# Inputs laid out feature-major, and Strassen over all 16 k tiles with uneven halves of the tokens, in a hybrid encoder layer on one core

## The chip, the cores and the metric

The kernel runs on one core of a Trainium2 chip. Its time is the device time of one execution in microseconds (us), as the median over several executions. The profile describes one execution, taken by the hardware profiler. PE is the matrix engine (PEld its weight loads), DVE the vector engine, ACT the scalar engine, POOL the GpSimd engine, SP the engine that issues most of the transfers. Each engine takes its instructions in the order in which they were issued to it, and waits on semaphores for what others make.

## The reference

One step of a hybrid layer for 544 tokens: 512 of a prompt and 32 of a running stream. All is float32. Cut to what matters:

```python
h = rmsnorm(x, g_norm)                     # 544 x 2048
proj = h @ w_in                            # 2048 x 6656, split by columns:
rq, rk, rv, rg, gu, gv, gg, aq, ag = split(proj)
ro = head_groupnorm(retention(rope(rq), rope(rk), rv, S0), g_ret) * silu(rg)   # 8 heads of 128
go = gu * (tril(w_s) @ layernorm(gv, g_gmlp) + b_s) * silu(gg)                 # 4 groups, chunks of 128
mk, mv = split(rmsnorm(mem, g_mem) @ w_mem_kv)                                 # 256 memory tokens
ao = softmax(aq @ mk.T * 128**-0.5) @ mv * silu(ag)                            # 4 heads
y = rmsnorm(x + concat(ro, go, ao) @ w_out, g_final)                           # w_out 2048 x 2048
# rmsnorm(x, g) = x * (mean(x*x) + 1e-6) ** -0.5 * g, the mean over the 2048 features
```

The outputs are y, the new retention states, the memory keys and values, and the normalised rows of gv of the 32 tokens.

## The kernel before

Everything is computed feature-major: features on the 128 partitions, tokens along the free axis. A block of 128 features is a k tile, and 2048 features are 16 of them. Every product runs in three passes for accuracy: `split` (L76, L79) writes a float32 tile as hi + lo, ACT copies the hi part and DVE subtracts to get the lo part, and PE multiplies hi·hi, hi·lo and lo·hi.

The two projections are cut into 34 pairs of column tiles of 128: xa0 to xa3 (queries and gates of the cross-attention), qk and vg 0 to 7 (retention), gv0, gv1, gg0 to gg3 (gating), o0 to o7 (output). For a pair, `project` applies Winograd's form of Strassen's algorithm: the 2 × 2 blocks are the two halves of k, the two column tiles, and the two halves of the tokens, 272 each (`TH`). It covers 12 of the 16 k tiles, six in each half (`KS`); the other four are multiplied plainly (`multiply_rest`, L183). So a pair is seven products of 6 × 3 = 18 matmuls and four plain ones of 4 × 3 = 12, all with 272 columns. The pairs xa0 and o0 run plainly while sums of token blocks are made (S1 to S4, called CS in the output projection). Each product has a PSUM bank of its own, and DVE adds the products together in SBUF. Units of the weight ("11", "21", "t4", ...: blocks of the weight and their sums) are split one step ahead of their use by `ahead`, on ACT and DVE.

The inputs lie in memory as the reference has them. Memory, x, keys, spatial weights and gains are transposed on PE (L401, L433, L479, L768, L493). At the end `residual` transposes the output back (L847), adds x, and `gather` sums its squares (ACT with accumulation, L863). All norms over features are therefore taken with tokens on the partitions: the factor of 128 tokens is one column of 128 values, and `rsqrt` (L121) raises 1 to 5 columns to the power −0.5 on POOL. The factors are then scalars by partition (L425, L884).

The tail: `first_tokens` finishes tokens 0 to 255 in the middle of the product t3 of o7, the rest after the last product. The time of the program is set by the order in which the code issues work to each engine's queue; there is no planner besides.

Of the kernel before, what the change touches and what calls it, by code (L numbers as in the profile page):

```python
# [14 lines left out]
P = 128  # L15
# [5 lines left out]
TH = T // 2  # L21
# [5 lines left out]
DH = 128  # L27
C_RQ, C_RK, C_RV, C_RG = 0, 1024, 2048, 3072
# [38 lines left out]
def step_kernel(ctx: ExitStack, tc: tile.TileContext, a, o):  # L67
    nc = tc.nc
    xp = a["x_prompt"][0]
    xs = a["x_sample"][0]  # L70
    w_in = a["w_in"][0]
    w_out = a["w_out"][0]
    w_kv = a["w_mem_kv"][0]
# [46 lines left out]
    def rsqrt(out, in_, n):  # L120
        nc.gpsimd.tensor_tensor(out=out, in0=in_, in1=mhalf[0:n, 0:in_.shape[1]], op=ALU.pow)  # L121
# [8 lines left out]
    turn = [0]  # L130

    # ---- weights
    def load_weight(src, c0, c1, name, between=None, halves=None):
        parts = []
        for i, (k0, k1) in enumerate(((0, KS), (KS, K2), (K2, KT))):
            r = wp.tile([P, k1 - k0, 2, P], F32, tag="raw" if i < 2 else "rawr", name=f"w{name}_{i}", bufs=3 if i < 2 else 2)
            rows = src[k0 * P:k1 * P, :]
            if between is not None:
                step = 3 if i < 2 else KR
                for u in range(0, k1 - k0, step):  # L140
                    between(k0 + u, k0 + u + step)
                    nc.sync.dma_start(out=r[:, u:u + step].rearrange("p k b c -> p k (b c)"),
                                      in_=rows[u * P:(u + step) * P, c0:c0 + 2 * P].rearrange("(k p) c -> p k c", p=P))
            elif halves:
                # runs of rows, the k tiles of the spatial gating last
                for u, k, n in (((0, 0, KS),), ((0, 6, 2), (2, 12, 4)), ((0, K2 - KR, KR),))[i]:
                    nc.sync.dma_start(out=r[:, u:u + n].rearrange("p k b c -> p k (b c)"),
                                      in_=src[k * P:(k + n) * P, c0:c0 + 2 * P].rearrange("(k p) c -> p k c", p=P))
            elif c1 == c0 + P:
                nc.sync.dma_start(out=r.rearrange("p k b c -> p k (b c)"),  # L150
                                  in_=rows[:, c0:c0 + 2 * P].rearrange("(k p) c -> p k c", p=P))
            else:
                for b, c in enumerate((c0, c1)):
                    nc.sync.dma_start(out=r[:, :, b, :], in_=rows[:, c:c + P].rearrange("(k p) c -> p k c", p=P))
            parts.append(r)
        return parts
# [5 lines left out]
    def rest_unit(r, name):
        hi = wp.tile([P, KR, 2, P], F32R, tag="rhi", name=f"h_{name}", bufs=1)
        lo = wp.tile([P, KR, 2, P], F32R, tag="rlo", name=f"l_{name}", bufs=1)
        split(hi, lo, r)
        return hi, lo

    def passes(w, x):
        return ((w[0], x[0]), (w[0], x[1]), (w[1], x[0]))

    def multiply(ps, w, x, start, stop, middle=None):
        """one block: KS k tiles, one column tile of the weight, half of the tokens"""
        for k in range(KS):
            if middle and k == KS // 2:
                middle()
# [24 lines left out]
    def ahead():  # L200
        if pending:
            pending.pop(0)()
# [782 lines left out]
```

## Time and profile before

| | |
|---|---|
| median of 3 executions | 938.05 us (937.85 to 938.76) |
| the profiled execution, first to last instruction | 932.9 us |
| mean granted TensorE clock | 0.995 |

The span is the profiled execution's own time on the core; what the device time holds beyond it lies around the program. A busy share says how long an engine had work; a group's row gives line, engine, operation, output<-input, shapes and count, then busy time, the mean of one in ns, and the idle time ahead of it with what ended it. In a timeline's row stand start, duration, engine, line, operation and shape, and, in brackets, the idle time ahead and its releaser. Matmuls overlap in the array, so the distance of two starts, not the duration of one, is what a matmul costs in a run of them.

### The profile page before, as it was taken

What the parts mean: (1) busy time and instruction counts of PE and PEld (TensorE: products, weight loads), DVE (VectorE), ACT (ScalarE), POOL (GpSimd) and SP (SyncE); (2) the same over time, 40 slices, a digit from 0 to 9 for tenths busy, and PEclk for the clock granted to TensorE, in tenths of its full rate; (3) what the DMA queues carried; (4) which work ended last, traced back from release to release, by engine and by line L of the source; (5) the groups of instructions that cost most, each with busy time, mean ns of one, the idle gap of its engine ahead of it and who ended that gap; (6) DMA issues with size and microseconds to landing.
All of it is one profiled execution on the core that took longest, in us unless ns stands there. A gap on an engine that the chain in (4) does not pass through costs nothing.

```text
span 932.9 us, 17496 instructions
## 1 busy us (share of the span) xinstructions
PE 910.6 (98%) x7145; PEld 887.4 (95%) x7145; DVE 712.2 (76%) x1200; ACT 423.9 (45%) x692; POOL 23.4 (3%) x26
## 2 busy tenths in 40 slices
PE   7999999999999999999999999999999999999994
PEld 6899999899999999999999999999999999999994
DVE  6789776667686869778686868678988987777774
ACT  6696443444343444444353434434434744443333
POOL 0210000000000000000000000001000000000000
PEclk9999999999999999999999999999999999999998
DMA  9884443133233332422232333344567993333205
GB/s 314 285 218 116 137 127 95 43 105 92 78 103 100 103 97 84 113 77 85 84 91 78 106 96 103 97 137 115 166 203 239 316 303 106 103 109 100 78 13 192
DMA packets 156832, 121.44 MB, mean 130 GB/s; under 512 B 5352, under 2 KB 149072, under 8 KB 156208
## 3 DMA queue, kind: packets, MB, share of 16 engines
q1 hardware_dynamic: 156096, 119.13, 41.9%
q10 hardware_dynamic: 656, 1.19, 0.4%
q8 instruction: 56, 0.92, 0.4%
q14 instruction: 24, 0.20, 0.1%
HBM read 105.93 MB, written 14.37 MB: 129 GB/s over the span
## 4 chain that ended last, share of the span: by engine, by line
PE 90%; DVE 3%; DMA 2%; ACT 2%; issue 1%; POOL 1%; POOLq 0%; DVEq 0%; ACTq 0%
PE xa0p L177 2%; PE o0p L177 2%; PE xa2p L177 2%; PE xa3p L177 2%; PE qk0p L177 2%; PE xa1p L177 2%; PE gv0p L177 2%; PE qk5p L177 2%; PE qk2p L177 2%; PE qk6p L177 2%; PE qk7p L177 2%; PE qk4p L177 2%; PE qk3p L177 2%; PE qk1p L177 2%; PE vg0p L177 2%; PE vg5p L177 2%
## 5 line engine op out<-in xcount | busy, mean ns | idle before, releaser
L472 PE MATMUL kvA<-h_kv,mm 128*128 128x256 f32 x96 | 26.2, 293 | 0.0
L472 PE MATMUL kvB<-h_kv,mm 128*128 128x256 f32 x96 | 25.4, 285 | 0.0
L121 POOL TENSOR_TENSOR stats<-stats,mhalf 128x5 f32<-128x5 f32 x8 | 9.4, 1170 | 540.3 <-DVE stats L704 347.2
L863 ACT ACTIVATE junk<-zp 128x256 bf16<-128x256 f32 (+1 forms) x36 | 13.7, 382 | 13.4 <-DVE zp L79 13.4
L472 PEld LDWEIGHTS kvA<-h_kv,mm 128*128 128x128 f32 x96 | 18.6, 194 | 0.2
L472 PEld LDWEIGHTS kvB<-h_kv,mm 128*128 128x128 f32 x96 | 18.5, 193 | 0.0
L79 DVE TENSOR_TENSOR l_kv<-wkv,h_kv 128x768 fp32r<-128x768 f32 x16 | 15.1, 951 | 2.4 <-ACT h_kv L76 2.4
L76 ACT ACTIVATE h_kv<-wkv 128x768 fp32r<-128x768 f32 x16 | 13.1, 835 | 5.6 <-DMA wkv<-in_w_mem_kv 2.8
L79 DVE TENSOR_TENSOR zp<-yp,zp 128x512 f32<-128x512 f32 (+1 forms) x18 | 11.1, 623 | 5.0 <-PE yp L847 4.3
L570 ACT ACTIVATE pr<-sc,st 128x256 f32<-128x256 f32 (+1 forms) x20 | 9.0, 466 | 12.6 <-DVE st L567 12.6
L693 PE MATMUL po<-vN,sT 128*128 128x128 f32 (+1 forms) x80 | 14.2, 276 | 0.0
L79 DVE TENSOR_TENSOR cats<-cats 128x272 f32<-128x272 f32 x24 | 10.5, 439 | 4.3 <-DMA cats<-cat 4.1
L472 PE MATMUL kvA<-l_kv,mm 128*128 128x256 f32 x48 | 13.6, 284 | 0.0
L712 DVE TENSOR_SCALAR on<-po,stats 128x128 f32<-128x128 f32 (+1 forms) x40 | 13.3, 401 | 0.3
L472 PE MATMUL kvB<-l_kv,mm 128*128 128x256 f32 x48 | 13.6, 283 | 0.0
L79 DVE TENSOR_TENSOR Xqk<-Xqk,cs 128x544 f32<-128x544 f32 x16 | 11.6, 725 | 1.9 <-ACT sw_q L76 1.9
L79 DVE TENSOR_TENSOR raw<-ps_x,gall 128x768 f32<-128x768 f32 (+3 forms) x12 | 8.1, 718 | 5.9 <-PE ps_x L433 5.9
L696 PE MATMUL po<-S,Xqk 128*128 128x128 f32 (+1 forms) x64 | 12.5, 277 | 0.0
L433 PE MATMUL ps_x<-ct,x 128*128 128x128 f32 (+1 forms) x80 | 10.1, 266 | 2.2 <-DVE x L425 2.0
L678 PE MATMUL pu<-vN,kN 128*128 128x128 f32 (+1 forms) x80 | 11.7, 284 | 0.0
L82 DVE SCALAR_TENSOR_TENSOR S<-S,pu 128x128 f32<-128x128 f32 x32 | 8.5, 286 | 3.9 <-ACT S L76 3.3
L678 PEld LDWEIGHTS pu<-vN,kN 128*128 128x128 f32 (+1 forms) x80 | 10.2, 189 | 1.0
(2289 smaller groups left out, 4190.2 us busy)
## 6 DMA issues: line engine op xcount, KB each, us to landing
wqk<-in_w_in SPq DMA_DIRECT2D x32, 384.0 KB, 4.4
wvg<-in_w_in SPq DMA_DIRECT2D x32, 384.0 KB, 4.3
wo<-in_w_out SPq DMA_DIRECT2D x16, 512.0 KB, 4.2
wxa<-in_w_in SPq DMA_DIRECT2D x16, 384.0 KB, 4.4
wgg<-in_w_in SPq DMA_DIRECT2D x16, 384.0 KB, 5.0
wo<-in_w_out SPq DMA_DIRECT2D x8, 768.0 KB, 4.8
wkv<-in_w_mem_kv SPq DMA_DIRECT2D x6, 768.0 KB, 7.6
x<-in_x_prompt SPq DMA_DIRECT2D x4, 1024.0 KB, 10.5
```

The costliest lines, as they stand in the source:

```text
L76: nc.scalar.activation(out=out, in_=in_, func=AF.Copy, scale=scale)
L79: nc.vector.tensor_tensor(out=out, in0=in0, in1=in1, op=op)
L121: nc.gpsimd.tensor_tensor(out=out, in0=in_, in1=mhalf[0:n, 0:in_.shape[1]], op=ALU.pow)
L177: nc.tensor.matmul(ps[:, 0:TH], lhsT=ww[:, k, :], rhs=xx[:, k, :], start=start and k == 0 and j == 0, stop=stop and k == KS - 1 and j == 2)
L433: nc.tensor.transpose(pv[:, k - k0, 0:n], x[0:n, k * P:(k + 1) * P], ident[0:n, 0:n])
L472: nc.tensor.matmul(ps[m][:, 0:256], lhsT=mm_[k // 3][:, k % 3, mi, ms], rhs=w[ww][:, kk, :], start=(k == 0 and j == 0), stop=(k == KT - 1 ...
L570: nc.scalar.activation(out=pr[0:n, t, :], in_=ps[0:n, (t - t0) * MEM:(t - t0 + 1) * MEM], func=AF.Exp, bias=st[0:n, 0, t:t + 1], scale=DH ...
L678: nc.tensor.matmul(pu[:, t * P:(t + 1) * P], lhsT=kN[0:n, t, :], rhs=v[0:n, t, :], start=True, stop=True)
L693: nc.tensor.matmul(po[0:n, t * P:(t + 1) * P], lhsT=sT[0:n, t * P:t * P + n], rhs=v[0:n, t, :], start=True, stop=(t == 0))
L696: nc.tensor.matmul(po[0:n, t * P:(t + 1) * P], lhsT=q[:, t * P:t * P + n], rhs=S[:, t - 1 if t < 4 else 4, :], start=False, stop=True)
L712: nc.vector.tensor_scalar(out=on[0:n, t, :], in0=po[0:n, t * P:(t + 1) * P], scalar1=s_[0:n, t, 0:1], scalar2=s_[0:n, t, 4:5], op0=ALU.sub ...
L863: nc.scalar.activation(out=junk[0:n, 0:n_ * P], in_=zp[:, t, fs] if t < 4 else zs, func=AF.Square, accum_out=ss[t // 2 > 0][0:n, t, u:u + 1])
```

## The change

The host now lays out the inputs: memory and x with features on the partitions, each half of a pair's weights as one contiguous megabyte, the keys and spatial weights transposed, the gains as columns. The output y leaves feature-major, and the host turns it back. All transposes of those on PE are gone (those of retention and gating stay).

Strassen covers all 16 k tiles, eight in each half, and `multiply_rest` is gone. The halves of the tokens are 256 (`N1`) and 288 (`N2`): blocks 11, 12 and S4 have 256 columns, 21, 22, S1, S2 and S3 have 288. A pair is seven products of 8 × 3 = 24 matmuls. The sums of products are accumulated on PE in two PSUM banks, Y and X; ACT copies the values that are needed in between.

```diff
-TH = T // 2
+N1 = 256
+N2 = T - N1
+KS = 8
-KS = 6                  # k tiles of each half of the part of K that is multiplied in seven products
-K2 = 2 * KS             # the other k tiles are multiplied plainly
...
     def rsqrt(out, in_, n):
-        nc.gpsimd.tensor_tensor(out=out, in0=in_, in1=mhalf[0:n, 0:in_.shape[1]], op=ALU.pow)
+        nc.gpsimd.tensor_tensor(out=out, in0=in_, in1=mhalf[0:n, 0:1].to_broadcast([n, in_.shape[1]]), op=ALU.pow)
...
+    SIZE = {"11": N1, "12": N1, "S4": N1, "21": N2, "22": N2, "S1": N2, "S2": N2, "S3": N2}
...
+                nc.sync.dma_start(out=w[half].rearrange("p k b c -> p (k b c)"), in_=a["w"][i, half])
...
+        product(y, name, "11", "11", True)
+        u1 = part(f"{name}u1")
+        copy(u1[:, 0:N1], y[:, 0:N1])
         next(other, None)
-        tt(d11, u2, block("21", "12", (0, 0)), ALU.add)
+        product(x, name, "21", "12", True)
+        tt(x0[:, 0:N1], u1[:, 0:N1], x[:, 0:N1], ALU.add)
         next(other, None)
-        copy(d21, block("t4", "22", (0, 1)))
+        product(y, name, "t2", "S2", False)
+        u2 = part(f"{name}u2")
+        copy(u2[:, 0:N1], y[:, 0:N1])
         next(other, None)
-        copy(d22, block(None, None, (1, 1)))
+        z = acc("X", f"{name}z")
+        product(z, name, "t1", "S1", True)
+        p5 = part(f"{name}p5")
+        copy(p5, z[:, 0:N2])
         next(other, None)
-        tt(u2, u2, block("t2", "S2"), ALU.add)
+        product(y, name, "t3", "S3", False)
+        tt(x1[:, N1:T], p5, y[:, 0:N2], ALU.add)
+        load_half(i + 1, 1)
         next(other, None)
-        tt(d12, u2, block("22", "S4", (1, 0)), ALU.add)
+        product(z, name, "22", "S4", False)
+        tt(x1[:, 0:N1], u2[:, 0:N1], z[:, 0:N1], ALU.add)
         next(other, None)
...
+        product(y, name, "t4", "22", False)
+        copy(x0[:, N1:T], y[:, 0:N2])
```

With features on the partitions the mean of squares runs over partitions and k tiles. ACT squares (`Square`), DVE halves the k tiles by additions (`halve`), and PE multiplies by a 128 × 128 tile of ones (`column_sums`), which leaves the sum of a token in every partition. `mean_rsqrt` scales it (DVE, L262) and takes the power on POOL (`rsqrt`, now L120), for all tokens of a half at once, in all 128 partitions. So the factor is a row that DVE multiplies in.

```diff
+    def column_sums(ps, parts):
+        for i, x in enumerate(parts):
+            nc.tensor.matmul(ps, lhsT=ones, rhs=x, start=i == 0, stop=i == len(parts) - 1)
+
+    def mean_rsqrt(out, ps, n):
+        nc.vector.tensor_scalar(out=out, in0=ps, scalar1=1.0 / D, scalar2=EPS, op0=ALU.mult, op1=ALU.add)
+        rsqrt(out, out, n)
...
+            def norm_mem():
+                parts = [x for s in sq for x in halve(s, KS)]
+                ps = small("rm_ps")
+                column_sums(ps[:, 0:MEM], parts)
...
+                mean_rsqrt(rm_bc, ps[:, 0:MEM], P)
+                mean_rsqrt(rm, ps[:, 512:514], P)
...
+                if g == 0:
+                    norm_mem()
+                for h in range(2):
+                    tt(mkT_p[:, 2 * g + h], ps[h][:, 0:MEM], rm_bc, ALU.mult)
...
+        def finish(t0, t1):
+            n = t1 - t0
+            ps = small(f"fin{t0}")
+            column_sums(ps[:, 0:n], [ss[:, c, t0:t1] for c in range(2)])
+            r = part(f"r{t0}")[:, 0:n]
+            mean_rsqrt(r, ps[:, 0:n], P)
+            for k in range(0, KT, 4):
+                z = zT[:, k:k + 4, t0:t1]
+                tt(z, z, r.unsqueeze(1).to_broadcast([P, 4, n]), ALU.mult)
+                nc.sync.dma_start(out=o["y"][:, k:k + 4, t0:t1], in_=z)
...
+                product(y, name, "t3", "S3", False)
+                add(1, 1, y)
+                finish(0, N1)
+                product(y, name, "t4", "22", False)
+                add(0, 1, y)
+                squares(fp, N1, T)
+                finish(N1, T)
```

Three places of the new order. First POOL, whole, but for its start and the groups of retention and gating; before, the powers of the start (st_m of memory, st_x of the tokens) and of the end (fin):

```order
L121 TENSOR_TENSOR st_m_318<-st_m_318,mhalf 128x1
L121 TENSOR_TENSOR st_m_326<-st_m_326,mhalf 128x1
L121 TENSOR_TENSOR st_x_338<-st_x_338,mhalf 128x1
L121 TENSOR_TENSOR st_x_371<-st_x_371,mhalf 128x1
L121 TENSOR_TENSOR st_x_542<-st_x_542,mhalf 128x1
```

And now, to the first of retention's (stats):

```order
L120 TENSOR_TENSOR rm_bc<-rm_bc,mhalf 128x256
L120 TENSOR_TENSOR rm<-rm,mhalf 128x2
L120 TENSOR_TENSOR r_bc<-r_bc,mhalf 128x256
L120 TENSOR_TENSOR r_bc<-r_bc,mhalf 128x288
L120 TENSOR_TENSOR stats_1754<-stats_1754,mhalf 128x5
```

Seven powers of one column (five shown) became three of 256 and 288 columns and one of two; at the end r0 and r256 have 256 and 288 in place of two and three.

DVE at the start, where memory keys are made. Before (wkv are loaded weights, h_kv and l_kv their halves, x0 the first 128 tokens):

```order
L79 TENSOR_TENSOR l_kv10_405<-wkv1_0_311,h_kv10_404 128x768
L384 TENSOR_SCALAR st_m1_326<-st_m1_326 128x1
L79 TENSOR_TENSOR l_kv11_427<-wkv1_0_311,h_kv11_426 128x768
L79 TENSOR_TENSOR l_kv12_449<-wkv1_1_313,h_kv12_448 128x768
L79 TENSOR_TENSOR l_kv1r_493<-wkv1_2_315,h_kv1r_492 128x1024
L384 TENSOR_SCALAR st_x0_338<-st_x0_338 128x1
L425 TENSOR_SCALAR x0_336<-x0_336,st_x0_338 128x2048
L79 TENSOR_TENSOR l_kv13_471<-wkv1_1_313,h_kv13_470 128x768
```

The same place now (wk1 are the weights of the second two heads' keys, sq11 squares of the first tokens; kY0 and kX0 are the sums in PSUM; the multiplies into mkT_p take what POOL makes of rm_bc):

```order
L262 TENSOR_SCALAR rm_bc_96<-rm_ps_249 128x256
L262 TENSOR_SCALAR rm_97<-rm_ps_249 128x2
L83 TENSOR_TENSOR l_k100_273<-wk1_0_264,h_k100_272 128x1024
L83 TENSOR_TENSOR mkT_p_85<-kY0_113,rm_bc_96 128x256
L83 TENSOR_TENSOR mkT_p_85<-kX0_114,rm_bc_96 128x256
L83 TENSOR_TENSOR l_k104_301<-wk1_0_264,h_k104_300 128x1024
L83 TENSOR_TENSOR l_k110_329<-wk1_1_267,h_k110_328 128x1024
L83 TENSOR_TENSOR sq11_396<-sq11_396 128x512
```

Where the factor was taken, a product's lo halves stood ahead of the instruction that uses it, and that was of x; now one lo half (l_k100) stands ahead of the multiplies by rm_bc and the others behind. Further down, the same holds for raw11 (behind r_bc of 256) and raw21 (behind r_bc of 288), with the splits of values and token blocks behind them.

DVE at the end, before (o7p are products in PSUM, Xo7 the pair's result, zp the output, fin the factors):

```order
L874 TENSOR_SCALAR fin0_10640<-fin0_10640 128x2
L884 TENSOR_SCALAR zp_8536<-zp_8536,fin0_10640 128x1024 x2
L79 TENSOR_TENSOR Xo7_10427<-o7u2_10432,o7p255_10663 128x272
L79 TENSOR_TENSOR Xo7_10427<-Xo7_10427,o7p256_10695 128x272
L79 TENSOR_TENSOR zp_8536<-yp14_2_10713,zp_8536 128x2x128
```

And now, to the end of DVE's order (o7y is the sum in PSUM, zT the output, ss the sums of squares):

```order
L262 TENSOR_SCALAR r0_9484<-fin0_9481 128x256
L83 TENSOR_TENSOR zT_7613<-zT_7613,r0_9484 128x4x256 x4
L83 TENSOR_TENSOR zT_7613<-o7y_9291,zT_7613 128x288
L83 TENSOR_TENSOR ss_7614<-ss_7614,sq70256_9521 128x288
L83 TENSOR_TENSOR ss_7614<-ss_7614,sq71256_9525 128x288
L262 TENSOR_SCALAR r256_9532<-fin256_9529 128x288
L83 TENSOR_TENSOR zT_7613<-zT_7613,r256_9532 128x4x288 x4
```

In both orders the multiplies by the first half's factors stand ahead of the addition of the last product; they are four of 1024 elements now, on DVE alone, where two were on DVE and two on ACT.

More of the change, by code (lines that the diff above doesn't have):

```diff
@@ L129, in step_kernel @@
     A = {}
[L130 to L156, printed above, removed]
@@ L162, in rest_unit @@
[L162 to L171, printed above, removed]
-        for k in range(KS):
-            if middle and k == KS // 2:
-                middle()
-            for j, (ww, xx) in enumerate(passes(w, x)):
-                nc.tensor.matmul(ps[:, 0:TH], lhsT=ww[:, k, :], rhs=xx[:, k, :],
-                                 start=start and k == 0 and j == 0, stop=stop and k == KS - 1 and j == 2)
@@ L180, in multiply_rest @@
-    def multiply_rest(ps, w, b, g, start, stop):
-        for k in range(KR):
-            for j, (ww, xx) in enumerate(passes(w, A["R"])):
-                nc.tensor.matmul(ps[:, 0:TH], lhsT=ww[:, k, b, :], rhs=xx[:, k, g * TH:(g + 1) * TH],
-                                 start=start and k == 0 and j == 0, stop=stop and k == KR - 1 and j == 2)
-    def ready(src, name):
-        u = unit(name)
-        split(u[0], u[1], src)
-        return u
-    pairs = {}
-    order = []
-    pending = []
@@ L195, in load_pair @@
-    def load_pair(i):
-        if i < len(order) and "raw" not in pairs[order[i]]:
-            w = pairs[order[i]]
-            w["raw"] = load_weight(*w["columns"], order[i], halves=order[i].startswith("o"))
-    def ahead():
-        if pending:
-            pending.pop(0)()
-    def enqueue(name, src, c0, c1, steps):
-        w = pairs[name] = {"columns": (src, c0, c1)}
-        at = len(order)
-        order.append(name)
-        def run(step):
-            load_pair(at)
-            step(name, w, *w["raw"])
-        pending.extend(lambda s=s: run(s) for s in steps)
@@ new lines, in step_kernel @@
+            keys(0)
+            for b in ("11", "12"):
+                load_x(b)
+            keys(1)
+            nc.sync.dma_start(out=o["cache_k"], in_=mkT_p)
+            nc.scalar.dma_start(out=ct, in_=a["table"][:, 0:K_COS])
+            v = values()
+            next(v)
+            for b in ("21", "22"):
+                load_x(b)
+            norm_x(0)
+            for _ in v:
+                pass
+            nc.sync.dma_start(out=o["cache_v"].rearrange("(m p) c -> p m c", p=P), in_=mv_p)
@@ L786, in normalise @@
[L786 to L790 removed]
+                nc.tensor.transpose(pv[0:n, g * P:(g + 1) * P], gvT[g][:, t * P:t * P + n], ident)
+            bn = pg.tile([P, 12], F32, tag="bn", name=f"gbn{t}", bufs=2)
+            nc.vector.bn_stats(out=bn[0:n, 0:6], in_=pv[0:n, 0:512])
+            nc.vector.bn_aggr(out=bn[0:n, 6:8], in_=bn[0:n, 0:6])
+            nc.vector.tensor_scalar(out=bn[0:n, 8:9], in0=bn[0:n, 7:8], scalar1=EPS, scalar2=None, op0=ALU.add)
```

821 lines of the change are left out of this document (373 added, 448 removed).

## The prediction, made before the changed kernel was run

> **What bounds the kernel now.** I read the page's busy shares first, then windows of 20 us, the list of waits, and single instructions.
>
> ```profile
> span 932.9 us, 17496 instructions
> PE 910.6 (98%) x7145; PEld 887.4 (95%) x7145; DVE 712.2 (76%) x1200; ACT 423.9 (45%) x692; POOL 23.4 (3%) x26
> 0.00:20.00 20.00, 13.67 (x90) 12.62 (x91) 11.39 (x17) 12.64 (x18) 0.76 (x5) 1.00 0.92 299
> 20.00:40.00 20.00, 17.63 (x149) 16.86 (x148) 16.16 (x23) 13.10 (x19) 3.82 (x3) 1.00 0.86 303
> 820.00:840.00 20.00, 20.00 (x163) 19.98 (x162) 16.57 (x25) 8.65 (x19) 0.00 (x0) 1.00 0.33 102
> 920.00:940.00 20.00, 0.23 (x3) 0.00 (x0) 4.75 (x13) 4.44 (x15) 0.85 (x1) 0.74 0.48 180
> ```
>
> A window's row gives busy time for PE, PEld, DVE, ACT and POOL, then granted clock, DMA share and GB/s. PE is full from about 40 us (20.00 of 20 at 820) until 920; only the first 40 us lose (20 − 13.67) + (20 − 17.63) = 8.7 us, and the last 12.7 us of the span hold no PE work. So PE sets the time, and an edit pays if it takes PE rows away, and costs if it makes PE wait. DVE has slack in the products (16.57 of 20), but little.
>
> **The change, part by part.** My own time for the sum is the span of 932.9; the median of 938.05 is 5.15 more, which lies around the span and stays.
>
> *Products.* Rows of the timeline, at full PE, ends of two even runs:
>
> ```profile
> 779.85 0.29 PE L183 MATMUL o1p<-CRh,h_o1r 128*128 128x272 f32 x1
> 783.12 0.29 PE L177 MATMUL o2p<-C11h,l_o2b 128*128 128x272 f32 x1
> 59.92 0.28 PE L472 MATMUL kvA<-l_kv,mm 128*128 128x256 f32 x1
> 61.62 0.28 PE L472 MATMUL kvB<-l_kv,mm 128*128 128x256 f32 x1
> 64.77 0.28 PE L472 MATMUL kvB<-h_kv,mm 128*128 128x256 f32 x1
> 66.19 0.28 PE L472 MATMUL kvB<-h_kv,mm 128*128 128x256 f32 x1
> ```
>
> Starts lie 26 matmuls apart in the first pair, 15 and 12 in the others: 272 columns take 3.27/26 = 125.8 ns, 256 take 113.3 to 118.3. No row has 288. From below it costs no more than 272 does (126); from above the line through 113.3 at 256 and 125.8 at 272 gives 138.3. I take it in proportion to 272, 133 ns, and 256 at 116, the middle of its two runs. A pair of column tiles was seven products of 18 matmuls plus four plain ones of 12: 126 + 48 = 174 at 125.8 = 21.89 us. It becomes seven of 24: three with 256 tokens and four with 288, 72 × 0.116 + 96 × 0.133 = 21.12. That is −0.77 for each of 32 pairs, −24.6, and −0.5 for the two plain pairs: **−25** (bounds −54 and −2, by cheapest and dearest pair of prices). The multiplications fall by 3%, but Strassen is bought on uneven halves.
>
> *Transposes gone.* Of x (80), of the output (80), of memory (32) and 21 small ones (keys, spatial weights, gains): 213 by the count in the code.
>
> ```profile
> 783.25 1.25 PE L847 MATMUL yp<-ct,Xo 128*128 128x128 f32 x10
> L433 PE MATMUL ps_x<-ct,x 128*128 128x128 f32 (+1 forms) x80 | 10.1, 266 | 2.2 <-DVE x L425 2.0
> L847 PE MATMUL yp<-ct,Xo 128*128 128x128 f32 (+1 forms) x80 | 10.4, 273 | 0.2 <-DVE Xo L79 0.2
> L401 PE MATMUL ps_m<-ct,mem 128*128 128x128 f32 x24 | 5.7, 392 | 1.6 <-DMA mem<-in_mem_prompt 1.6
> ```
>
> Ten take 1.25, of which the last's latency is 0.28: 0.108 each, so −23; those of the start ran slower (L401: 5.7 for 24), and by the three groups' busy time, 26.2 for 184, it would be −30. PE is the bound in most of it: **−24** (−23 to −30).
>
> *Column sums added.* The squares of memory and tokens are summed over partitions by plain fp32 matmuls against ones: five calls of two inputs or fewer, each matmul two passes as in this row (7.8 us for 32 records):
>
> ```profile
> L561 PE MATMUL sc<-mkT_p,Xxa 128*128 128x256 f32 x32 | 7.8, 382 | 0.0
> ```
>
> At 0.24 us a record, five sums × 2 × 2: **+5**.
>
> *The start without POOL.* The new start is long on DVE:
>
> ```profile
> L79 DVE TENSOR_TENSOR l_kv<-wkv,h_kv 128x768 fp32r<-128x768 f32 x16 | 15.1, 951 | 2.4 <-ACT h_kv L76 2.4
> L79 DVE TENSOR_TENSOR zp<-zp,gz 128x1024 f32<-128x1024 f32 x7 | 8.5, 1219 | 0.0
> ```
>
> A 1024-wide operation takes 1.22 us (951 × 1024/768 = 1.27 by the other row). Each memory chunk needs three (scale, subtract, subtract of the weight) = 3.7 us against 24 × 0.116 = 2.8 of PE; halving the squares of two tiles is 2 × (1.22 + 0.61 + 0.31) = 4.3; and around xa0 the sums of blocks and their splits are 24 such widths, 30 us, against 8 × 24 matmuls, 24 us, of PE. Together I put this at **+18**: the four chunks' lag, 3.6; the halvings of memory and of the first tokens, 8; xa0's 6. Loads bring the same bytes in longer runs; where DMA is near full (0.92 in the first row) that may help, and it is left at 0. Hand-overs between PSUM banks in retention and gating, where a product now waits for DVE to read the bank before it accumulates on, **+10**. Bounds for both together 0 (all beside other work, as at 820) and 35 (none beside).
>
> *The end without POOL.* Now PE's end and the span's lie 12.7 us apart. After it: an add, squares, sums, a tensor_scalar, four multiplies of 1152 columns (1.22 × 1152/1024 = 1.4 each) and the stores, about the same: 0.
>
> Sum so far: 932.9 − 25 − 24 + 5 + 18 + 10 = **917**.
>
> *Five wide pows.* The reciprocal root stands on POOL still, but it is now taken of rows that are spread over all partitions: 256, 256, 288, 256 and 288 columns, 1344 in all, where it was 1 to 5.
>
> ```profile
> 647.49 0.55 POOL L121 TENSOR_TENSOR gbn<-gbn,mhalf 128x1 f32<-128x1 f32 x1 [3.25 <-DVE gbn L779]
> 915.50 0.70 POOL L121 TENSOR_TENSOR fin<-fin,mhalf 128x2 f32<-128x2 f32 x1 [261.86 <-DVE fin L874]
> 922.58 0.85 POOL L121 TENSOR_TENSOR fin<-fin,mhalf 128x3 f32<-128x3 f32 x1 [6.37 <-DVE fin L874]
> 354.61 1.17 POOL L121 TENSOR_TENSOR stats<-stats,mhalf 128x5 f32<-128x5 f32 x1 [49.71 <-DVE stats L704]
> 355.82 0.23 DVE L707 TENSOR_SCALAR stats<-stats,ct 128x5 f32<-128x5 f32 x1 [1.35 <-POOL stats L121]
> ```
>
> One column takes 0.55, two 0.70, three 0.85, five 1.17: a straight line of (1.17 − 0.55)/4 = 0.155 us a column on 0.4 of fixed time, and DVE waits for the end (355.82). By that line 256 columns take 0.55 + 255 × 0.155 = 40.1 us and 288 take 45.0; three and two of them 210. From below: nothing for a further column, 0.55 each, 3 in all. The four rows are all there is, they are straight, and I take 0.155.
>
> What hides it? DVE works in order, and behind each instruction that takes the factor stand the lo halves that PE's next products need. In the order of after these are the multiplies into mkT_p, raw11 and raw21, and those by r0 and r256 at the end. PE has one product to do past each: 2.8 us (the second keys' first chunk), nothing sure in the values, 2.8 (xa0's first), 3.2 (the last product, 24 × 0.133), nothing at the end: 9. The fourth pow ends after that last product, whose add stands on DVE behind the four multiplies by r0; only then come the squares, sums and pow of the other half. So 40.1 and 45.0 are in series. 210 − 9 = +201. After each of the first three waits PE starts cold, which the granted clock of the rows does not show:
>
> ```profile
> 9.50:13.10 3.60, 3.60 (x18) 3.30 (x17) 3.17 (x4) 2.95 (x4) 0.00 (x0) 1.00 1.08 365
> ```
>
> 18 matmuls took 3.6 us, 0.2 each against 0.116, some 1.6 a restart: +5. **+206**, and 917 + 206 + 5.15 = 1128; I say **1130**.
>
> The Trainium skill (GPSIMD Engine Reference, section 3.1, Elementwise) puts a two-input elementwise operation at about 2.6 cycles an element, and an add of 2048 columns at 4497 ns. My estimate from that page would be 4497/2048 = 2.2 ns a column, some 1.1 us for each wide pow, and a time of about 925. The narrow rows above speak against it for pow, 155 ns a column, but no row before has more than five columns.
>
> POOL can also be held by DVE:
>
> ```profile
> 35.63 0.95 DVE L79 TENSOR_TENSOR l_kv<-wkv,h_kv 128x768 fp32r<-128x768 f32 x1
> 35.80 1.19 POOL L121 TENSOR_TENSOR st_x<-st_x,mhalf 128x1 f32<-128x1 f32 x1 [4.91 <-DVE st_x L384]
> ```
>
> The same one column took 1.19 instead of 0.55, while a subtraction of two SBUF tiles ran. If the opposite holds too, that a long pow stops such subtractions, l_k100, queued behind the first factor's scaling, comes only after it, and the first cover of 2.8 is lost: within the rounding. The Trainium skill (SBUF — State Buffer, section "SBUF: two separate sides") calls this an exclusive lock on a shared port pair, held for a whole instruction; the two rows agree with it in one direction, and by it the sum would be 3 more.
>
> **The rivals.**
> *Wide pow is cheap* (the other sign). If further columns cost 12 ns or less, the five pows take under 19 us, half of it covered; the point where it decides is (938 − 922)/1344 = 12 ns a column, uncovered. For it: an operation may have a slow fixed path for a few columns and another for many; nothing wider was seen. Against: a line exact from one to five. At nothing a column, 917 + 3 + 5 = 925 (905 with two thirds of the way to the products' lower bound; 935 with 35 in place of 28 for start and hand-overs, and 3 for the lock).
> *Something between* 12 and 140 ns, with a wide operation cheaper by vectors: 940 to 1100.
> *The products don't shorten*: at 138.3 and 118.3 a pair is 72 × 0.1183 + 96 × 0.1383 = 21.79, −2 in all, and with a cheap pow 925 + 23 = 948. Against: it asks for two dear prices at once. With a dear pow it only moves 1130 to 1153.
>
> **How the numbers follow.** The line of 0.155 holds: 0.58, 1130, with its own range 1100 (products −54) to 1160 (products −2, start 35). Between: 0.13. Cheap pow: 0.21, 925. Products that don't shorten with a cheap pow: 0.05, slower. The two cancelling to within 0.2%, about what a measurement here can tell from none: 0.03. Faster 0.21, same 0.03, slower 0.58 + 0.13 + 0.05 = 0.76. Without the cheap pow the range would leave out over 2 in 10, so it reaches down to that: 905 to 1160.
>
> **What would show it.** POOL's five wide instructions at 40 to 45 us each, with DVE's wait for rm_bc, r_bc, r0 and r256 as long, and PE idle in three gaps of 35 us or more in the first 200 us; two such gaps in series at the end. Product spacings of 0.116 and 0.133 in the middle, and no transposes in it. I am wrong if a wide pow takes under 15 us, or if PE is busy beside it.

## The result, and the profile after

| | before | after |
|---|---|---|
| median | 937.95 us (4 runs, 935.72 to 938.76) | 1153.66 us (4 runs, 1151.99 to 1155.67) |
| ratio | | 1.2305, 95% interval 1.2281 to 1.233 |
| span of the profiled execution | 932.9 | 1153.9 |

The change makes the kernel 23% slower; 1130 was forecast. The medians differ by 215.7 us, the two profiled spans by 221.0. The profiled execution of the kernel before was a short one: in its 37 later executions the span is 932.5 to 938.3 us, 936.1 in the middle, and the device time only 1.7 to 1.9 us more. So differences to 932.9 below come out some 3 us large.

The page of the changed kernel, its head and two rows of the 40 slices:

```profile
span 1153.9 us, 15985 instructions
PE 893.3 (77%) x6672; PEld 860.6 (75%) x6672; DVE 730.7 (63%) x1038; ACT 430.5 (37%) x606; POOL 232.3 (20%) x23
PE   5050350899999999999999999999999899993000
POOL 0959369000000000000000000010000000007796
```

PE's busy time fell by 17 us, from 910.6 to 893.3, but it is 77% of a longer span. The holes in PE's row stand where POOL's row is full: three in the first 8 slices of 29 us, and the end. The timeline of POOL alone, start and duration in us, names what fills them:

```profile
27.66 42.10 POOL L120 TENSOR_TENSOR rm_bc<-rm_bc,mhalf 128x256 f32<-128x256 f32 x1 [27.22 <-DVE rm L262]
83.26 41.13 POOL L120 TENSOR_TENSOR r_bc<-r_bc,mhalf 128x256 f32<-128x256 f32 x1 [12.84 <-DVE r_bc L262]
155.03 46.22 POOL L120 TENSOR_TENSOR r_bc<-r_bc,mhalf 128x288 f32<-128x288 f32 x1 [30.64 <-DVE r_bc L262]
1046.83 41.13 POOL L120 TENSOR_TENSOR r<-r,mhalf 128x256 f32<-128x256 f32 x1 [262.09 <-DVE r L262]
1097.01 46.23 POOL L120 TENSOR_TENSOR r<-r,mhalf 128x288 f32<-128x288 f32 x1 [9.05 <-DVE r L262]
```

Together 216.8 us, where the straight line through one to five columns had given 210. The list of waits (us in total, times, longest) carries it on to DVE and from there to PE:

```profile
DVE zT L83 <- POOL r L120: 87.7, 2, 46.4
DVE raw L86 <- POOL r_bc L120: 85.7, 2, 44.5
DVE mkT_p L83 <- POOL rm_bc L120: 41.0, 1, 41.0
PE fin L259 <- DVE ss L83: 44.7, 1, 44.7
PE xa0p L205 <- ACT A21h L80: 44.3, 1, 44.3
PE vY L393 <- ACT h_v L80: 41.5, 1, 41.5
PE kY L371 <- DVE l_k L83: 41.2, 2, 40.0
```

The first three rows are DVE on POOL. The four behind them are PE on something near to it: PE's releaser is DVE or ACT, never POOL. Who reads PE's rows alone sees no power at all; the chain has to be followed two engines back. While it lasts, the windows of 20 us (PE, PEld, DVE, ACT, POOL, granted clock, DMA share, GB/s) show every engine but POOL at nothing and PE's clock at half:

```profile
100.00:120.00 20.00, 0.00 (x0) 0.00 (x0) 0.00 (x0) 0.00 (x0) 20.00 (x1) 0.50 0.00 0
1060.00:1080.00 20.00, 0.00 (x0) 0.00 (x0) 0.00 (x0) 0.00 (x0) 20.00 (x1) 0.50 0.00 0
```

The products themselves, from PE's timeline at full speed in the middle of retention:

```profile
615.70 0.30 PE L205 MATMUL vg5y<-A22l,h_vg5t 128*128 128x288 f32 x1
618.63 0.29 PE L205 MATMUL vg5y<-A22h,l_vg5t 128*128 128x288 f32 x1
618.76 0.28 PE L205 MATMUL qk6y<-A11h,h_qk 128*128 128x256 f32 x1
621.62 0.28 PE L205 MATMUL qk6x<-A12h,h_qk 128*128 128x256 f32 x1
```

22 steps in 2.93 us are 133.2 ns at 288 columns; 24 in 2.86 are 119.2 at 256. With 125.8 at 272 that is 0.463 to 0.466 ns a column at all three sizes. A pair is now 72 × 0.1192 + 96 × 0.1332 = 21.37 us against 21.89.

By stage, from the start of the last matmul of the named pair in the timelines (narrow: the first experiment, in which the powers are narrow and nothing else is changed but an earlier load of a table):

| us from that of the stage before | before | after | narrow | narrow − before |
|---|---|---|---|---|
| start to xa0 | 95.6 | 227.7 | 103.1 | +7.5 |
| xa1 | 28.9 | 33.3 | 33.5 | +4.6 |
| xa2, xa3 | 56.2 | 55.2 | 55.1 | −1.1 |
| retention (16 pairs) | 407.3 | 403.1 | 403.3 | −4.0 |
| gv, gg (6 pairs) | 144.3 | 146.2 | 145.1 | +0.8 |
| o0 | 25.6 | 26.3 | 26.0 | +0.4 |
| o1 | 23.0 | 28.3 | 28.7 | +5.7 |
| o2 to o6 | 114.6 | 106.7 | 106.7 | −7.9 |
| o7 | 23.4 | 22.3 | 23.8 | +0.4 |
| from there to the end | 14.0 | 104.8 | 20.5 | +6.5 |
| span | 932.9 | 1153.9 | 945.8 | +12.9 |

The 221 us lie in the first row (+132) and the last (+91). Everything between gains 2 us in all. Of the 12.9 at the bottom, the medians (947.48 and 938.03) show 9.5; the rest comes with the short span of the kernel before.

### The profile page after: what moved, and what is told of

It is laid out like the page before. It is cut to its first block, busy times and chain, and to the rows that moved or that the text cites. A ratio compares the mean times of both kernels' runs of the same rounds, so it can differ in the third digit from the quotient of the medians.

```text
span 1153.9 us, 15985 instructions
## 1 busy us (share of the span) xinstructions
PE 893.3 (77%) x6672; PEld 860.6 (75%) x6672; DVE 730.7 (63%) x1038; ACT 430.5 (37%) x606; POOL 232.3 (20%) x23
## 4 chain that ended last, share of the span: by engine, by line
PE 56%; DVE 11%; POOL 5%; POOLq 4%; DMA 3%; issue 2%; ACT 1%; DVEq 0%; SPq 0%; ACTq 0%
POOLq L891 4%; POOL r L120 4%; DMA cats<-cats 1%; PE xa3y L205 1%; PE xa2y L205 1%; PE qk0y L205 1%; PE o2y L205 1%; PE o6y L205 1%; PE o5y L205 1%; PE o4y L205 1%; PE o3y L205 1%; PE vg0y L205 1%; PE vg4y L205 1%; PE vg1y L205 1%; PE vg6y L205 1%
## 5 line engine op out<-in xcount | busy, mean ns | idle before, releaser
L120 POOL TENSOR_TENSOR r<-r,mhalf 128x256 f32<-128x256 f32 (+1 forms) x2 | 87.4, 43680 | 271.1 <-DVE r L262 271.1
L120 POOL TENSOR_TENSOR stats<-stats,mhalf 128x5 f32<-128x5 f32 x8 | 9.4, 1171 | 533.8 <-DVE stats L617 344.3
L120 POOL TENSOR_TENSOR r_bc<-r_bc,mhalf 128x256 f32<-128x256 f32 (+1 forms) x2 | 87.3, 43672 | 43.5 <-DVE r_bc L262 43.5
L120 POOL TENSOR_TENSOR rm_bc<-rm_bc,mhalf 128x256 f32<-128x256 f32 x1 | 42.1, 42096 | 27.2 <-DVE rm L262 27.2
L393 PE MATMUL vY<-h_v,mm 128*128 128x512 f32 x32 | 14.4, 450 | 41.5 <-ACT h_v L80 41.5
L80 ACT ACTIVATE h_qk<-wqk 128x1024 fp32r<-128x1024 f32 x24 | 25.4, 1059 | 52.0 <-PE vg0z L205 3.1
L83 DVE TENSOR_TENSOR l_qk<-wqk,h_qk 128x1024 fp32r<-128x1024 f32 x24 | 29.3, 1220 | 22.6 <-ACT h_qk L80 22.6
L80 ACT ACTIVATE h_vg<-wvg 128x1024 fp32r<-128x1024 f32 x24 | 25.3, 1055 | 48.3 <-PE qk2z L205 4.2
L80 ACT ACTIVATE h_o<-wo 128x1024 fp32r<-128x1024 f32 x25 | 26.5, 1060 | 36.9 <-PE o0p L205 5.0
L205 PE MATMUL xa0p<-A21h,h_xa 128*128 128x288 f32 x16 | 5.0, 324 | 44.3 <-ACT A21h L80 44.3
L259 PE MATMUL fin<-ss,ones 128*128 128x256 f32 (+1 forms) x8 | 3.3, 550 | 44.7 <-DVE ss L83 44.7
L83 DVE TENSOR_TENSOR l_o<-wo,h_o 128x1024 fp32r<-128x1024 f32 x25 | 30.5, 1222 | 6.9 <-ACT h_o L80 6.9
L83 DVE TENSOR_TENSOR l_vg<-wvg,h_vg 128x1024 fp32r<-128x1024 f32 x24 | 29.3, 1221 | 3.5 <-ACT h_vg L80 3.5
```

The source lines that it names most:

```text
L80: nc.scalar.activation(out=out, in_=in_, func=AF.Copy, scale=scale)
L83: nc.vector.tensor_tensor(out=out, in0=in0, in1=in1, op=op)
L120: nc.gpsimd.tensor_tensor(out=out, in0=in_, in1=mhalf[0:n, 0:1].to_broadcast([n, in_.shape[1]]), op=ALU.pow)
L205: nc.tensor.matmul(ps[:, 0:n], lhsT=ww[:, k, :], rhs=xx[:, k, :], start=start and k == 0 and j == 0, stop=k == KS - 1 and j == 2, skip_gro ...
L259: nc.tensor.matmul(ps, lhsT=ones, rhs=x, start=i == 0, stop=i == len(parts) - 1)
L393: nc.tensor.matmul(ps[m], lhsT=mm[k // KS][mi][:, k % KS, ms], rhs=w[wi][:, kk], start=(k == 0 and j == 0), stop=(k == KT - 1 and j == 2))
```

## The experiments

The forecast blamed five powers on POOL. Its rivals were a loss by the new structure itself, and POOL locking DVE out. "Ratio" is always to the kernel before, on the same chip; three chips were used, and the kernel before takes 938.0, 937.7 and 938.3 us on them.

**1. Narrow powers.** Only how the factor is made changes: one matmul per 128 tokens sums the squares into a column with tokens on the partitions, POOL raises 2 or 3 columns, and PE spreads them with ones times a diagonal. The table that holds the identity for this is loaded earlier.

```diff
-            column_sums(ps[:, 0:n], [ss[:, c, t0:t1] for c in range(2)])
-            mean_rsqrt(r, ps[:, 0:n], P)
+            row_rsqrt(r, ps, [ss[:, c, t0:t1] for c in range(2)], n, ...)
+    def row_rsqrt(out, ps, parts, n, s):
...
+                nc.tensor.matmul(ps[0:w, 512 + m:513 + m], lhsT=x[:, m * P:m * P + w], rhs=ones[:, 0:1], ...)
+            mean_rsqrt(s[0:w, c0:c1], ps[0:w, 512 + c0:512 + c1], w)
...
+            nc.vector.tensor_scalar(out=d, in0=ident[0:w, 0:w], scalar1=s[0:w, m:m + 1], ...)
+            nc.tensor.matmul(ps[:, m * P:m * P + w], lhsT=ones[0:w, :], rhs=d, start=True, stop=True)
+        copy(out, ps[:, 0:n])
```

> Only the width of the five powers is changed: PE sums the squares of a token into one column of 2 or 3 (tokens on the partitions), POOL raises those, and PE spreads them over the partitions again. Theory A (the price per column of a power on POOL is the loss, and PE waits for it in full): the five powers shrink from 217 us to about 4, PE's five gaps of 40 to 46 us vanish, and each factor keeps a chain of small steps of some 3 us: 935 to 955 us, a ratio of 1.00 to 1.02 to before. Theory B (the new structure loses by itself: the order on DVE, banks handed over, uneven halves): the gaps shrink but 1000 us or more stay.

947.48 us, ratio 1.0089 (1.0062 to 1.0116). The width of the powers costs 1153.66 − 947.48 = 206 us by the medians, 1153.9 − 945.8 = 208 by the spans. The rest of the change is no gain either: 0.9% slower.

**2. Square root on ACT, reciprocal on DVE**, at the full width.

```diff
+        if out.shape[1] > 5:
+            nc.scalar.activation(out=out, in_=out, func=AF.Sqrt)
+            nc.vector.reciprocal(out=out, in_=out)
```

> The five wide powers are replaced in place, with the same 256 and 288 columns, by a square root on ACT and a reciprocal on DVE; all else is the changed kernel. Theory A (POOL's price, not the width as such): the ACT and DVE operations take about 0.4 to 2 us each instead of 41 to 46, 930 to 955 us. Theory B (any wide factor in DVE's queue is dear): over 1000.

952.84 us, ratio 1.016 (1.0145 to 1.0176). So a wide factor in DVE's order is not dear as such; it is dear from POOL. The reciprocal of 256 columns takes 1.75 us on DVE, the root 0.4 on ACT.

**3. Powers beside other work.** On the kernel of experiment 2, six powers and a multiplication on POOL.

```diff
+        for m, n in ((P, 8), (P, 32), (P, 64), (P, 128), (32, 256), (P, 256)):
+            nc.gpsimd.tensor_tensor(out=pr1[0:m, 0:n], in0=pr0[0:m, 0:n], in1=mhalf[0:m, 0:1].to_broadcast([m, n]), op=ALU.pow)
+        nc.gpsimd.tensor_tensor(out=pr1, in0=pr0, in1=mhalf[:, 0:1].to_broadcast([P, 256]), op=ALU.mult)
```

> The kernel with the square root, and beside it on POOL, which is then idle, six powers that nobody waits for (8, 32, 64 and 128 columns on 128 partitions, 256 on 32 partitions, 256 on 128) and a multiplication of 256 columns. A straight line in the columns: 1.7, 5.5, 10.5, 20.5 and 41 us, and 41 on 32 partitions if the price goes by column, about 10 if it goes by element. If a wide path exists only for plain operations, the multiplication takes about 1 us. If POOL's operation locks DVE out for its whole length, DVE's subtractions stall for some 100 us in all and the time rises by that; if not, it stays within 1% of the kernel with the square root.

POOL's groups by shape (busy us, mean ns), a subtraction on DVE from the timeline in the same stretch, and a row of the waits:

```profile
L280 POOL TENSOR_TENSOR probe_out<-probe_in,mhalf 128x256 f32<-128x256 f32 x1 | 41.1, 41117 | 0.1
L280 POOL TENSOR_TENSOR probe_out<-probe_in,mhalf 32x256 f32<-32x256 f32 x1 | 41.1, 41106 | 0.1
L280 POOL TENSOR_TENSOR probe_out<-probe_in,mhalf 128x128 f32<-128x128 f32 x1 | 26.9, 26872 | 0.1
L280 POOL TENSOR_TENSOR probe_out<-probe_in,mhalf 128x64 f32<-128x64 f32 x1 | 10.5, 10522 | 0.1
L280 POOL TENSOR_TENSOR probe_out<-probe_in,mhalf 128x32 f32<-128x32 f32 x1 | 5.4, 5430 | 0.1
L280 POOL TENSOR_TENSOR probe_out<-probe_in,mhalf 128x8 f32<-128x8 f32 x1 | 1.7, 1651 | 1.2 <-DVE probe_out L276 1.2
L281 POOL TENSOR_TENSOR probe_out<-probe_in,mhalf 128x256 f32<-128x256 f32 x1 | 0.6, 613 | 0.1
65.20 1.23 DVE L83 TENSOR_TENSOR l_v<-wv,h_v 128x1024 fp32r<-128x1024 f32 x1 [0.76 <-ACT h_v L80]
ACT mv_p L80 <- POOL rm L120: 56.6, 1, 56.6
```

The line holds from 8 to 256 columns, 0.157 to 0.159 us each; only the power of 128, beside dense work of DVE, takes 27 where the line gives 21. 32 partitions cost what 128 do, so the price goes by column. A multiplication of 256 columns takes 0.6 us: it is the power, not POOL, that is dear. DVE's subtraction of two SBUF tiles still takes 1.23 us in the middle of the power of 41 on 32 partitions: no lock. (Experiment 4 shows the same on 128 partitions.) The time rose all the same, to 1011.23 (one run), and there the expectation was wrong: somebody did wait, the small power of the memory's second factor (rm), queued on POOL behind the six, and ACT's scaling of the values behind it. In the code the six stand far behind that power; on POOL they came ahead of it.

**4. Keys scaled late.** With wide powers on POOL, ACT takes the keys' sums out of PSUM and the multiplies by rm_bc are written behind the tokens.

```diff
-                    tt(mkT_p[:, 2 * g + h], ps[h][:, 0:MEM], rm_bc, ALU.mult)
+                    copy(mkT_p[:, 2 * g + h], ps[h][:, 0:MEM])
...
             block("21", raw["21"])
+            for h in range(XH):
+                tt(mkT_p[:, h], mkT_p[:, h], rm_bc, ALU.mult)
```

> POOL's wide powers stay. ACT takes the keys' sums out of PSUM unscaled, and DVE multiplies them by the memory's factor only after all tokens are normalised: no instruction that PE needs stands behind the first factor any more. If DVE's order is what makes PE wait, the first gap of 40 us goes. By that alone -40 (1113). But the second power then starts when the first ends, at about 70 instead of 83 us, since POOL takes one after the other: by POOL's order the gain is only about 13 (1140). If a power on POOL stops DVE by itself, no gain (1153).

1142.99 us (one run), the span 12.7 shorter, near the 13 by POOL's order. But DVE's timeline shows that the experiment did not do what it was to do:

```profile
26.78 42.10 POOL L120 TENSOR_TENSOR rm_bc<-rm_bc,mhalf 128x256 f32<-128x256 f32 x1 [26.34 <-DVE rm L262]
32.92 1.23 DVE L83 TENSOR_TENSOR l_k<-wk,h_k 128x1024 fp32r<-128x1024 f32 x1 [0.59 <-ACT h_k L80]
68.91 0.43 DVE L83 TENSOR_TENSOR mkT_p<-mkT_p,rm_bc 128x256 f32<-128x256 f32 x1 [33.83 <-POOL rm_bc L120]
```

In the code the multiplies now stand behind the split of raw21; in DVE's order they came out ahead of the values' first lo halves, and there they still hold DVE for 34 us. So the order in which the code is written is not the order on an engine, and the sentence ahead of the prediction that there is no planner besides is wrong: after each such edit the order has to be read in the timeline. The memory keys were done meanwhile, and PE's first gap fell from 40.0 to 28.6 us, which is most of the 12.7. This agrees with the reading that what PE gets done during a power is what stands ahead of it on DVE; POOL's order as a second limit stays untested. The second row shows again that the power, here on 128 partitions, leaves DVE's subtraction at full speed.

**5. Even halves**, on experiment 1.

```diff
-N1 = 256
+N1 = 272
```

> The kernel with narrow powers, and halves of 272 and 272 tokens instead of 256 and 288. If a product costs in proportion to its columns (119 ns at 256 and 133.3 at 288 in the trace of the changed kernel, 125.8 at 272 before), a pair falls from 72 x 0.119 + 96 x 0.1333 = 21.37 to 168 x 0.1258 = 21.13 us, -0.24 for each of 32 pairs: -8, 940 us (from 947.5). If the smaller half were the cheaper way, 947 or more. If what surrounds the products limits a pair, no change.

945.31 us, ratio 1.0081 (1.006 to 1.0103): −2.2 by the medians, whose intervals overlap; −5.9 by the profiled spans, of which experiment 5's is the shortest of its four. In the stages it is clearer: retention takes 400.9 us against 403.3, o2 to o6 105.8 against 106.7, 0.15 to 0.18 a pair where 0.24 was expected. In retention all profiled kernels with even halves have 400.9, all with uneven ones 403.1 to 403.3, so the gain in the products is real; the whole time is too close to tell.

**6, 7, 8. Sums of blocks on POOL**; the same with even halves; and the last product ahead of the first half's finish.

```diff
-                    tt(raw["22"], raw["21"], raw["22"], ALU.add)
+                    ptt(raw["22"], raw["21"], raw["22"], ALU.add)     # on POOL, and the three others
...
-                finish(0, N1)
                 product(y, name, "t4", "22", False)
+                finish(0, N1)
```

> The kernel with narrow powers, and the four sums of token blocks ahead of xa1 (9.4 us of DVE) made on POOL by plain additions and subtractions. In the kernel with narrow powers xa1 takes 40.5 us from its first product to xa2's, before 28.1. Theory A (DVE's backlog is what xa1 waits for): xa1 falls to 32 to 35 us and the time by 6 to 8, to 940. Theory B (xa1 waits for its weights or for ACT): no change. A rival on POOL: if its wide subtraction stops DVE's, or takes over 10 us each, the time rises.

> Even halves and sums on POOL together, with narrow powers. If both are independent, -8 and -7: 932, below before (938). If DVE's backlog eats the shorter products, 938 to 942.

> As the one before, and in the last pair PE takes the last product ahead of the first half's column sums. In the kernel with narrow powers PE waits 3.9 us for the sums of squares and 2.1 us for the factor ahead of that product. If these waits count, -3 to -5 against the kernel before it; if DVE's four multiplies set the end, 0.

Slower, all three: 954.49 (1.0179, 1.0158 to 1.0201), 955.1 (1.0199, 1.0175 to 1.0224) and 957.05 (1.0217, 1.02 to 1.0234). The timeline of the sixth says why, POOL first, then DVE:

```profile
103.77 5.47 POOL L86 TENSOR_TENSOR raw<-raw,raw 128x2048 f32<-128x2048 f32 x1 [2.57 <-DVE AS1l L83]
109.32 5.50 POOL L86 TENSOR_TENSOR raw<-raw,raw 128x2048 f32<-128x2048 f32 x1
104.75 5.58 DVE L83 TENSOR_TENSOR l_xa<-wxa,h_xa 128x1024 fp32r<-128x1024 f32 x1
110.36 5.55 DVE L83 TENSOR_TENSOR wxa<-wxa 128x1024 f32<-128x1024 f32 x1
```

Two of DVE's subtractions that take 1.22 us elsewhere begin inside POOL's plain subtractions, and each ends about 1.1 us after POOL's does. Plain wide operations on POOL do hold DVE; this is the rival's lock, at another operation. The sums themselves also take longer, 4.7 to 6.2 us each on POOL against 2.3 to 2.6 on DVE; how much of the loss is which was not separated. In the sixth it lies ahead of xa0's last matmul (112.9 us, 103.1 in the first), in the seventh at xa1 (46.1 us, 34.1 in the fifth).

The eighth is 2 us above the seventh, within their scatter. The last pair falls from 24.3 to 22.5 us, and the end grows from 20.2 to 22.6: PE now waits 5.9 us for the sums of squares, where in the first experiment it was 3.9. The new order only moves the wait. The expectation had also misplaced the waits: in the first experiment 0.7 us of them stand ahead of the last product, and the 3.9 and 1.4 behind it.

**9, 10. No halving on DVE; sums for the output earlier.** On experiment 5, PE sums all 16 k tiles by matmuls of one column; and on top of that, in the code, the sums of the last two k tiles stand among o0's products.

```diff
             def halve(x, k):
-                while k > 1:
-                    k //= 2
-                    tt(x[:, 0:k], x[:, 0:k], x[:, k:2 * k], ALU.add)
                 return [x[:, i] for i in range(k)]
...
+                        if k == 0 and j in (0, 2):
+                            next(late)
```

> The kernel with narrow powers and even halves, without the additions by which DVE halves the squares: PE sums all 16 k tiles itself, one column at a time. That takes some 14 us from DVE in the first 80 us and adds 14 matmuls of one column to each of seven (token tile) sums, 98 or so, about 10 us of PE. If DVE's backlog is what PE waits for ahead of xa2 (136.8 us with halving, 124.7 before the change), xa2 starts at 126 to 131 us, and the time falls by 6 to 10: 936 to 939. If PE's own work or the loads set that stage, 0 or up to +10.

> As the one before, and the sums of the last two k tiles for the output projection are made during o0 instead of behind its products. In the kernel with even halves PE waits 5.4 us for ACT's copy of the block S2 at o1, since the block's load comes behind those sums. If that order is the cause, -4 to -6 against the kernel before it: 931 to 934, below before (938). If the transfers are the limit at that place (DMA share 1.05 there), 0 to -1.

965.54 (1.03, 1.0276 to 1.0323) and 966.26 (1.03, 1.0275 to 1.0324): misses. Windows of the ninth, and its sum of the first tokens in PE's timeline:

```profile
20.00:40.00 20.00, 20.00 (x137) 20.00 (x137) 1.47 (x4) 5.63 (x6) 0.70 (x1) 0.75 0.62 254
33.69 11.89 PE L269 MATMUL r_ps<-ones,sq 128*128 128x1 f32 x96
```

The sums cost PE 12 us at one place, in DVE's order everything behind them waits (1.47 busy of 20), and the granted clock falls to 0.75 although PE is "busy" all the time. So this says nothing on DVE's backlog.

In the tenth PE's wait for S2 at o1 is still there (7.5 us, 5.6 in the ninth). But the edit did not do what it was to do either. DVE's last sums for the output, in the ninth and then in the tenth, whose first products of o0 start at 754.8 and 756.2:

```profile
778.16 1.87 DVE L83 TENSOR_TENSOR cats<-cats 128x272 f32<-128x272 f32 x4 [0.50 <-issue]
780.74 1.87 DVE L83 TENSOR_TENSOR cats<-cats 128x272 f32<-128x272 f32 x4 [2.26 <-issue]
```

They start 23.4 and 24.5 us behind that product: they did not become earlier, and whether their order is the cause of the wait was not tested.

**11. Sums left out**, on experiment 1: the four sums of token blocks, nothing in their place.

> The kernel with narrow powers (halves of 256 and 288) without the four sums of token blocks ahead of xa1, which leaves the input projection's sums out (S1 to S4 are split as they lie): 9.4 us less on DVE, nothing put elsewhere. In the kernel with narrow powers PE waits 4.7 us for DVE's lo half of xa1 and runs cold behind it; xa0's last matmul starts at 103.1 and xa1's at 136.6, before at 95.6 and 124.5. If DVE's backlog is what the start loses, xa1's last matmul comes 6 to 10 us earlier (127 to 131) and the time is 938 to 942. If it is PE's own work or ACT, it stays within 2 us.

938.38 us, ratio 0.9998 (0.9988 to 1.0007), 9.1 less than with the sums, which take 9.4 us of DVE. xa1's last matmul starts at 129.1, inside the expected 127 to 131, and xa1 takes 26.6 us instead of 33.5; the rest of the 9.1 lies in gating, o1 and xa0, where it is no larger than the scatter between profiles. The windows behind xa0, with the sums and without:

```profile
96.00:110.00 14.00, 9.25 (x64) 8.71 (x63) 14.00 (x12) 7.78 (x9) 0.00 (x0) 0.84 0.39 150
96.00:110.00 14.00, 14.00 (x113) 13.90 (x111) 13.96 (x15) 9.75 (x12) 0.00 (x0) 1.00 0.29 118
```

DVE is full in both; with the sums PE has 4.75 us of nothing, a clock of 0.84 behind it, and without them it is full. PE's wait of 4.7 us for DVE's lo half is gone as well. DVE's backlog is the cause of the loss at xa1, shown by this run.

**12. x loaded later**, on experiment 5: each pair's x waits for the pair before.

```diff
+            if fp:
+                copy(zT[:, 2 * fp, 0:1], zT[:, 2 * fp - 2, 0:1])
             nc.sync.dma_start(out=zT[:, ks], in_=a["xT"][:, ks])
```

> The kernel with narrow powers and even halves, where x for the output projection's pairs is loaded one pair ahead instead of all at once: seven of eight loads of 544 KB leave the stretch in which o1 waits for the block S2 (5.4 us, DMA share 1.05 near it). If the crowded transfers are what o1 loses there, 4 to 6 us less: 939 to 941 (from 945.3). If S2 waits for the writes of its sums, no change.

949.72 us, ratio 1.0119 (1.0099 to 1.0138): a miss. PE no longer waits for S2 at o1 but for the addition of x:

```profile
PE o1y L205 <- DVE zT L83: 7.5, 1, 7.5
```

The load of x came too late instead; in the 20 us from 760 on, the DMA share is 0.95 with it and 1.03 in experiment 5. What o1 loses stays open. Crowded transfers alone hardly explain it: in the kernel before, the same stretch has shares of 0.96 and 0.90, and PE waits for nothing there. What differs is when the sums are made: the kernel before has the last of them 23 us ahead of o0's first product, the changed kernels 23 to 25 us behind it, and S2 can only be loaded after them. This is argued from the timelines, not tested. No version beat the kernel before.

## Why the prediction was right

**The powers: right in place, kind and size.** 0.155 us a column and +206 were forecast; 0.16 and 206 (208 by the spans) were measured. The four narrow rows were enough to carry a line fifty times further, and the cheap wide path, which had a chance of 0.21, did not show at up to 288 columns. The Trainium skill (GPSIMD Engine Reference, section 3.1, Elementwise) gives 4497 ns for an add of 2048 columns, by my estimate from that 2.2 ns a column. The multiplication of 0.6 us here, 2.4 ns a column, agrees with it, and the power is 67 times as dear.

**What hides them: that 206 came out is in part luck.** The sum let PE work for 9 us beside the powers and had no term for the way from a power back to PE. In the trace PE goes on for 4.0, 5.0, 5.1 and 2.6 us behind the start of the first four powers, 16.8 in all, more than forecast. But when they have ended, DVE's and ACT's instructions behind them keep PE waiting for another 2.0, 5.4, 3.1 and 6.2 us, 16.7 in all. The two cancel: PE's gaps in the list and the wait at the end are 40.0 + 41.5 + 44.3 + 44.7 + 46.4 = 216.9, the powers 216.8. At the end the halves are in series, by rows of DVE that stand behind each other as shown in the order:

```profile
1088.00 4.63 DVE L83 TENSOR_TENSOR zT<-zT,r 128x1024 f32<-128x1024 f32 x4 [41.31 <-POOL r L120]
1092.55 0.45 DVE L83 TENSOR_TENSOR zT<-o7y,zT 128x288 f32<-128x288 f32 x1
1143.27 5.16 DVE L83 TENSOR_TENSOR zT<-zT,r 128x1152 f32<-128x1152 f32 x4 [46.40 <-POOL r L120]
```

**The cold restarts** came where forecast, and somewhat larger. Behind the first gap some 15 matmuls of 256 columns stand 0.213 us apart before the distance falls to 0.119. With the first step that costs 1.6 us, and 2.9 and 1.9 behind the next two gaps: 6.4 in all, where 5 was forecast. Here the granted clock does show it, 0.50 behind the first gap:

```profile
71.70:75.00 3.30, 3.27 (x15) 3.27 (x16) 3.30 (x5) 0.00 (x0) 0.00 (x0) 0.50 0.62 216
```

**The lock: rejected for powers, real for plain operations.** The Trainium skill (SBUF — State Buffer, section "SBUF: two separate sides") has it as exclusive for a whole instruction. Experiment 6 agrees; experiments 3 and 4 do not, since a power of 41 us lets DVE's subtractions pass at full speed. Only one that began just behind the start of the third power, at 155.19, took 1.59 us instead of 1.22. The first power did not hold l_k100 back, so the 3 us more by that rule did not come at that place.

**The rest of the sum: 922 forecast (917 + 5.15), 947.5 measured with narrow powers.** Nearly the whole miss of 1130 against 1153.7 lies here. The terms one by one, by the table of stages (and so with the short span of the kernel before in them):
- *Products*, −25: 256 columns cost 119.2 ns, not 116. By −0.52 a pair they give −17. The whole gain of Strassen over 16 k tiles is 2.4% of a pair; the columns alone, 72 × 256 + 96 × 288 = 46080 against 174 × 272 = 47328, say 2.6.
- *Transposes*, −24, fit: in o2 to o6 a pair falls by 1.58, and −0.52 for the products leaves 1.06, ten transposes of 0.106.
- *The start*, +18, was right up to xa0: with 128 transposes less, two to three column sums and xa0's own −0.3 it came to some +7, and +7.5 was measured. Some of that agreement is chance: experiment 1's own steps are in the 7.5, and experiment 2, which has none of them, reaches that point 12.3 later than the kernel before. The last part, 6 for the sums of blocks, was too small: they hold xa1 too, which takes 4.6 more where 0.5 less was due, and falls by 6.8 without them (experiment 11).
- *Hand-overs*, +10: retention lost 16 × 0.52 − 4.0 = 4.3 and the gating 6 × 0.52 + 0.8 = 3.9 against the products' price, 8 in all. The gating's part is loose: that stage takes 142.6 to 146.2 us in the profiles with uneven halves.
- *Loads*, left at 0: o1 is 5.7 longer, where o2 to o6 fell by 1.58 each. Its wait for S2 is not in the sum, and its cause is open.
- *The end without POOL*, 0: 20.5 us in experiment 1 against 14.0. DVE's two times four multiplies (4.63 and 5.16) now stand in series where ACT took half. Experiment 1's own steps are not the reason: experiment 2 has none and needs 21.7.

**The 5.15 around the span** is a misreading, though a harmless one. It was taken as time that lies around every execution, but it is the distance of the median from one short profiled execution: in all 37 later executions of the kernel before the device time is 1.7 to 1.9 us above the span, as it is in the changed kernel (1155.67 − 1153.9 = 1.8). Adding it only brings the sum back from the span to the median, so the forecast of 1128 stands as 938.05 and the changes to it.

The rival of products that don't shorten, with a cheap power, had 948 us. Without the powers' width the kernel takes 947.5, 0.9% slower and not 1.4% faster as the sum with a cheap power said. But that number is met by chance: the products did shorten, by 0.52 us a pair, and the loss lies at xa1, o1 and the end.

## What to carry to other kernels

When a layout is turned, look at what becomes of the small tensors: a factor that was one column of 128 tokens became a row of 256 in each of 128 partitions, and an engine whose price goes by column took 41 us instead of 0.55. Carry a narrow price to a wide shape by a line through several widths before assuming that width is free, and move the narrow shape (PE can sum into columns and spread them again) rather than widen the dear operation. A saving on the bound engine is worth what the engines that feed it can follow: here some 41 us of PE work went (17 for the products, 24 for the transposes), and DVE at xa1, the wait at o1, the hand-overs and the end gave more than that back. And when an edit moves an instruction in the code, look in the timeline whether it moved on the engine: in two experiments here it did not come where it was meant to be.

## What the runs showed of the hardware

- A power on POOL: 0.16 us a column from 1 to 288 columns, the same on 32 and 128 partitions; a multiplication of 256 columns, 0.6 us.
- A power of 41 us on POOL lets DVE's two-input operations run at full speed (1.23 us); beside plain subtractions of 2048 columns on POOL (5.47 and 5.50 us) two of them took 5.58 and 5.55 and ended behind POOL's.
- Matmuls of three passes cost 0.463 to 0.466 ns a column at 256, 272 and 288 columns: a column costs the same in halves of any of these sizes.
- 96 matmul records of one column took 11.89 us, 0.124 each, as long as one of 256 columns in a product (0.119), and the granted clock fell to 0.75 in a window in which PE counts as fully busy.
- Behind a gap of 40 us, some 15 matmuls of 256 columns ran 0.213 us apart at a granted clock of 0.50, then 0.119 apart.
